# Two-layer trunk: one packed input for the front with three transfers in flight, a third raw buffer, rotating low halves, and the first norm in the fifth chunk

## The chip, the cores and the metric

The kernel runs on one core of one Trainium2 chip. The metric is the device time of one execution in microseconds (us). One profiled execution of the kernel before is read row by row; its times count from the start of its span. The engines are called by the names of the profile: PE is TensorE (matmuls; PEld is its weight load), DVE is VectorE, ACT is ScalarE, POOL is GpSimd, SP is SyncE, which here issues nearly all DMA transfers.

## The reference

The kernel computes a two-layer trunk on 256 tokens with 16 meta tokens ahead of them (272 positions), model width 2048, in float32:

```python
h = concat([meta, x])                                   # 272 x 2048
for i in range(2):
    hn = rms_norm(h, pre_norm_g[i])
    y = diff_attention(hn) if i == 0 else pool_mixer(hn)
    h = h + rms_norm(y, post_norm_g[i])
return h[16:]
# diff_attention: proj = hn @ w_in (2048 -> 8192: q, k, v, gate); 8 heads, two softmax maps each,
#   p1 - lam * p2, per-head norm, times silu(gate), @ w_out (2048 -> 2048)
# pool_mixer: proj = hn @ w_in (2048 -> 4096: u, gate); windowed means minus u, a grouped
#   512 x 512 matmul, times silu(gate), @ w_out
```

`rms_norm` divides by the root of the mean square over the 2048 features and scales by a learned vector.

## The kernel before

**Layout and arithmetic.** Activations lie transposed: features on the 128 partitions, 16 feature blocks (k = 0 to 15), 272 positions in the free dimension. Each float32 operand of a matmul is split into a high half (a cast to the reduced type float32r) and a low half (value minus high half); a product is then three matmuls: high by high, high by low, low by high (`mm3`, L119). Weights are read in chunks of 128 x 2048 (1 MB, `CW` = 2048): one chunk is 128 output features with all 16 k blocks. `load(i)` (L75) issues chunk i's transfer on SP into a ring of two raw buffers, `split(i)` (L84) makes the high half on ACT (L97) and the low half on DVE (L98), `take()` (L110) hands out chunk i, splits i + 1 and loads i + 2.

**The front.** The first four chunks (`FIRST`) are not read one after the other. They are packed with the activations: `first` has for each k the 272 activation columns and 4 x 128 weight columns (784 columns, 392 KB for one k). SP issues eleven pieces of it, all at once as far as its queue goes: k = 0 in two pieces (400 and 384 columns), k = 1, 2, 3 alone, then pairs (L216 to L219). The small table `sp` of learned vectors (70 columns, 35 KB) has a transfer of its own, issued by ACT (L140). For every k, ACT casts the weights (`fhi`, L243) and scales and casts the activations (`xs`, L247), DVE makes the low halves (`flo`, L244; the low part of `xs`, L248), and PE runs 12 matmuls: four chunks by three (L252 to L254), which accumulate in four banks `pq0` to `pq3`. I call the 12 matmuls of one k a slice. Before the data is there, PE runs a warm-up on a matrix of ones (`busy(6)`, L206; twelve passes in the trace). The low halves of the first eight k lie in one tile, those of the second eight in another.

**The first norm.** The pre-norm's row factor is applied after the projection, so the projection need not wait for it. ACT squares the activations in place (L237), DVE adds them up by halving (`fold`, L103; 4, 2 and 1 blocks at a time, L107; the sum of both eights at L268). PE then takes the mean over the partitions (`mean`, L177: the tile `rms_pre`), DVE adds epsilon (`v`, L182), POOL raises it to the power −0.5 (L183), DVE lays the result on a diagonal (`r`, L197), PE spreads it over all partitions (`spread`, L198), and DVE copies it out (`r0`, L275). In the kernel before, the mean stands in the sixth chunk (number 5, `pq5`) after 5 of its 16 k blocks, and the spread 25 matmuls later.

**What sets the order.** The program is written as one stream; the framework puts each engine's instructions into a queue of their own, in an order that its scheduler sets from modelled ready times, and adds the semaphores. `issue_after(x)` holds a block's instructions behind x on x's engine. An engine runs its queue strictly in order. A tile taken from a pool with `bufs=n` reuses the memory of the n-th one before it and waits until that is read. Behind the front come the other chunks of the first projection, eight heads of attention between them, the output projection, the second norm with the pooling layer's projections, and the last output with its norm.

Of the kernel before, what the change touches and what calls it, by code (L numbers as in the profile page):

```python
# [42 lines left out]
@with_exitstack  # L43
def trunk(ctx: ExitStack, tc: tile.TileContext, first, hT, xt, small, gpost1, rope, w_in, w_out, p_in, p_grp, p_out, out):
    nc = tc.nc
# [29 lines left out]
    def load(i, parts=1):  # L75
        if i >= NCH or i in raw:
            return
        t = wpool.tile([P, CW], F32, tag="raw", name=f"raw{i}", bufs=2)
        w = CW // parts
        for q in range(parts):  # L80
            nc.sync.dma_start(t[:, q * w:(q + 1) * w], chunks[i][:, q * w:(q + 1) * w])
        raw[i] = t
# [27 lines left out]
    def take(ahead=True):  # L110
        i = cur[0]
        cur[0] += 1
        split(i)
        if ahead:
            split(i + 1)
            load(i + 2)
        return halves[i]
# [14 lines left out]
    def busy(n):  # L132

        ps = bank("busy")
        for _ in range(n):
            pe.matmul(ps[:, 0:P], ones, ones, start=True, stop=True)
# [9 lines left out]
    ones = const.tile([P, P], F32, name="ones")  # L146
    pool.memset(ones, 1.0)
    warm = const.tile([P, 1], F32, name="warm")
    act.square(warm, ones[:, 0:1])
    ones_r = const.tile([P, P], F32R, name="ones_r")  # L150
# [54 lines left out]

    busy(6)  # L206
    x0 = ExitStack()
# [4 lines left out]
    NF = len(FIRST)  # L212
    pk = xp.tile([P, KT, L + NF * P], F32, name="pk")
    fhi = base.tile([P, KT, NF, P], F32R, tag="os", name="fhi")
    flo = (base.tile([P, KT // 2, NF, P], F32R, tag="big", name="flo0"), xp.tile([P, KT // 2, NF, P], F32R, name="flo1"))
    nc.sync.dma_start(pk[:, 0, 0:L + P], first[:, 0, 0:L + P])  # L216
    nc.sync.dma_start(pk[:, 0, L + P:], first[:, 0, L + P:])
    for a, b in ((1, 2), (2, 3), (3, 4), (4, 6), (6, 8), (8, 10), (10, 12), (12, 14), (14, 16)):
        nc.sync.dma_start(pk[:, a:b, :], first[:, a:b, :])  # L219
    load(NF)  # L220
    nc.sync.dma_start(rp, rope)
    load(NF + 1)
    acc0 = [bank(f"pq{i}") for i in range(NF + 2)]
# [15 lines left out]
    for k in range(KT):  # L239
        hi, lw = fhi[:, k], flo[k // 8][:, k % 8]  # L240
        for i, n in ((0, 1), (1, NF - 1)) if k == 0 else ((0, NF),):
            w = pk[:, k, L + i * P:L + (i + n) * P].rearrange("p (i c) -> p i c", c=P)
            act.copy(hi[:, i:i + n], w)  # L243
            dve.tensor_tensor(out=lw[:, i:i + n], in0=w, in1=hi.bitcast(F32)[:, i:i + n], op=ALU.subtract)  # L244
            if i == 0:
                g = sp[:, C_PRE0 + k:C_PRE0 + k + 1]
                act.activation(xh[:, k, :], pk[:, k, 0:L], AF.Copy, scale=g)  # L247
                dve.scalar_tensor_tensor(out=xl[:, k, :], in0=pk[:, k, 0:L], scalar=g, in1=xh.bitcast(F32)[:, k, :],  # L248
                                         op0=ALU.mult, op1=ALU.subtract)
        for i in range(NF):  # L250
            o = acc0[i][:, 0:L]
            pe.matmul(o, hi[:, i], xh[:, k, :], start=k == 0, stop=False)  # L252
            pe.matmul(o, lw[:, i], xh[:, k, :], start=False, stop=False)
            pe.matmul(o, hi[:, i], xl[:, k, :], start=False, stop=k == KT - 1)  # L254
# [32 lines left out]


    lp = const.tile([P, 2], F32, name="lp")
    dve.tensor_tensor(out=lp, in0=sp[:, C_LAM:C_LAM + 2], in1=sp[:, C_LAM + 2:C_LAM + 4], op=ALU.mult)  # L290
    psl = bank("psl")
    pe.matmul(psl[:, 0:2], ones, lp, start=True, stop=True)
    le = const.tile([P, 2], F32, name="le")
    act.activation(le, psl[:, 0:2], AF.Exp)
    dve.scalar_tensor_tensor(out=lamc, in0=le[:, 0:1], scalar=LAM_INIT, in1=le[:, 1:2], op0=ALU.add, op1=ALU.subtract)

# [220 lines left out]
    for slot in range(NH * 6 + KT):  # L517
        if slot < NH * 6:
            h, i = divmod(slot, 6)
            hd = heads[h]  # L520
            if i == 0:
                hd.h = h
                hd.qk = att.tile([P, 4, L], F32, name=f"qk{h}", tag="qk")
                hd.qs = att.tile([P, 2, 4, L], F32R, name=f"qs{h}", tag="qs")
                hd.qkh, hd.qkl = hd.qs[:, 0], hd.qs[:, 1]
                hd.qm = att.tile([P, 2, 2, 32], F32R, name=f"qm{h}", tag="qm")
                hd.sw = att.tile([ROPE, 4, L], F32, name=f"sw{h}", tag="sw")
                hd.vT = att.tile([P, 2, L], F32, name=f"vT{h}", tag="vT")
# [6 lines left out]
        if slot == NF + 2:  # L535
# [147 lines left out]
    def pooled(t, ps):  # L683
# [6 lines left out]
        while step < w:  # L690
# [219 lines left out]
```

## Time and profile before

| what | us |
|---|---|
| median of 3 runs (lowest, highest) | 837.18 (837.1, 837.63) |
| the profiled execution: its own time | 837.1 |
| its span, first to last instruction | 835.3 |
| outside the span | 1.8 |
| PE busy, share of the span | 827.9 (99%) |
| DVE busy | 584.9 (70%) |
| ACT busy | 437.4 (52%) |
| POOL busy | 5.3 (1%) |
| moved by DMA, mean rate | 149.35 MB, 179 GB/s |

PE is busy nearly always, so the few waits of PE matter and the sums of the other engines don't. A row of a timeline gives start, duration, engine, line, operation, tiles (out<-in) and shape; `x6` behind it joins rows that follow each other; in square brackets stand the idle time of the engine ahead of it and what ended it. Durations of matmuls overlap, since they are pipelined: what one costs in a row of equal ones is the distance from start to start. In a row of waits stand the waiting operation, the one waited for, the total, the count and the longest. A row of windows gives for each engine the busy time and, in brackets, the number of instructions.

### The profile page before, as it was taken

What the parts mean: (1) busy time and instruction counts of PE and PEld (TensorE: products, weight loads), DVE (VectorE), ACT (ScalarE), POOL (GpSimd) and SP (SyncE); (2) the same over time, 40 slices, a digit from 0 to 9 for tenths busy, and PEclk for the clock granted to TensorE, in tenths of its full rate; (3) what the DMA queues carried; (4) which work ended last, traced back from release to release, by engine and by line L of the source; (5) the groups of instructions that cost most, each with busy time, mean ns of one, the idle gap of its engine ahead of it and who ended that gap; (6) DMA issues with size and microseconds to landing.
All of it is one profiled execution on the core that took longest, in us unless ns stands there. A gap on an engine that the chain in (4) does not pass through costs nothing.

```text
span 835.3 us, 14459 instructions
## 1 busy us (share of the span) xinstructions
PE 827.9 (99%) x6060; PEld 796.5 (95%) x6060; DVE 584.9 (70%) x962; ACT 437.4 (52%) x681; POOL 5.3 (1%) x13
## 2 busy tenths in 40 slices
PE   9999999999999999999999999999999999999997
PEld 9999999999999999999999999999999888888886
DVE  6799767675868687897854644696998666685523
ACT  8656555454546465855344544654444545563422
POOL 0100000000000000000000000000000000000000
PEclk9999999999999999999999999999999999999999
DMA  9446344444444444345459744146457555545512
GB/s 355 171 151 206 149 157 156 163 160 160 164 153 153 151 151 151 132 179 194 154 189 371 277 179 151 51 176 211 172 204 266 196 190 202 178 174 203 201 50 101
DMA packets 22385, 149.35 MB, mean 179 GB/s; under 512 B 2608, under 2 KB 2992, under 8 KB 5552
## 3 DMA queue, kind: packets, MB, share of 16 engines
q1 hardware_dynamic: 22032, 148.14, 49.0%
q8 instruction: 47, 0.77, 0.4%
q10 hardware_dynamic: 288, 0.30, 0.1%
q14 instruction: 18, 0.15, 0.0%
HBM read 146.33 MB, written 2.10 MB: 178 GB/s over the span
## 4 chain that ended last, share of the span: by engine, by line
PE 98%; POOL 0%; DMA 0%; DVE 0%; ACT 0%; issue 0%; DVEq 0%; ACTq 0%; POOLq 0%
PE p L121 14%; PE p L123 14%; PE p L122 14%; PE pv L129 7%; PE py L121 4%; PE py L123 4%; PE py L122 4%; PE pu L121 4%; PE pu L122 4%; PE pu L123 4%; PE pv L130 4%; PE pz L780 4%; PE pz L779 4%; PE pz L781 3%; PE pm L129 2%; PE pq L252 1%
## 5 line engine op out<-in xcount | busy, mean ns | idle before, releaser
L98 DVE TENSOR_TENSOR lo<-raw,hi 128x2048 fp32r<-128x2048 f32 (+1 forms) x123 | 279.2, 2270 | 137.6 <-ACT hi L97 137.6
L97 ACT CAST hi<-raw 128x2048 fp32r<-128x2048 f32 (+1 forms) x123 | 232.9, 1895 | 188.6 <-PE p L122 96.3
L121 PE MATMUL p<-xs,hi 128*128 128x272 f32 x928 | 270.2, 291 | 0.0
L123 PE MATMUL p<-xs,lo 128*128 128x272 f32 x928 | 268.5, 289 | 0.0
L122 PE MATMUL p<-xs,hi 128*128 128x272 f32 x928 | 267.4, 288 | 0.0
L121 PEld LDWEIGHTS p<-xs,hi 128*128 128x128 f32 x928 | 174.7, 188 | 0.3
L122 PEld LDWEIGHTS p<-xs,hi 128*128 128x128 f32 x928 | 174.8, 188 | 0.0
L123 PEld LDWEIGHTS p<-xs,lo 128*128 128x128 f32 x928 | 174.6, 188 | 0.0
L129 PE MATMUL pv<-hs,hi 128*128 128x512 f32 x256 | 89.5, 393 | 0.0
L121 PE MATMUL py<-os,hi 128*128 128x272 f32 x256 | 74.3, 290 | 0.0
L123 PE MATMUL py<-os,lo 128*128 128x272 f32 x256 | 74.1, 289 | 0.0
L122 PE MATMUL py<-os,hi 128*128 128x272 f32 x256 | 73.7, 288 | 0.0
L130 PE MATMUL pv<-hs,lo 128*128 128x256 f32 x256 | 71.8, 280 | 0.0
L123 PE MATMUL pu<-hs,lo 128*128 128x260 f32 (+3 forms) x224 | 63.7, 285 | 0.0
L121 PE MATMUL pu<-hs,hi 128*128 128x260 f32 (+3 forms) x224 | 63.6, 285 | 0.0
L122 PE MATMUL pu<-hs,hi 128*128 128x260 f32 (+3 forms) x224 | 63.5, 284 | 0.0
L129 PEld LDWEIGHTS pv<-hs,hi 128*128 128x128 f32 x256 | 48.1, 188 | 10.9
L122 PEld LDWEIGHTS py<-os,hi 128*128 128x128 f32 x256 | 48.3, 189 | 0.0
L121 PEld LDWEIGHTS py<-os,hi 128*128 128x128 f32 x256 | 48.2, 188 | 0.0
L123 PEld LDWEIGHTS py<-os,lo 128*128 128x128 f32 x256 | 48.2, 188 | 0.0
L130 PEld LDWEIGHTS pv<-hs,lo 128*128 128x128 f32 x256 | 48.1, 188 | 0.0
L781 PE MATMUL pz<-hi,zs 128*128 128x512 f32 (+1 forms) x120 | 45.0, 375 | 0.0
(254 smaller groups left out, 1318.3 us busy)
## 6 DMA issues: line engine op xcount, KB each, us to landing
raw<-in_w_in SPq DMA_DIRECT2D x60, 1024.0 KB, 4.8
raw<-in_p_in SPq DMA_DIRECT2D x29, 1024.0 KB, 4.8
raw<-in_w_out SPq DMA_DIRECT2D x16, 1024.0 KB, 4.9
raw<-in_p_out SPq DMA_DIRECT2D x14, 1024.0 KB, 4.8
pk<-in_first SPq DMA_DIRECT2D x6, 784.0 KB, 10.6
raw<-in_p_grp SPq DMA_DIRECT2D x4, 1024.0 KB, 4.7
rawu<-in_p_in SPq DMA_DIRECT2D x3, 1024.0 KB, 5.3
h<-in_hT SPq DMA_DIRECT2D x4, 544.0 KB, 7.1
```

The lines of the kernel that those rows point to most:

```text
L97: act.copy(hi[:, s], raw[i][:, s])
L98: rest[i] = dve.tensor_tensor(out=lw[:, s], in0=raw[i][:, s], in1=hi.bitcast(F32)[:, s], op=ALU.subtract)
L121: pe.matmul(o, wh, xh, start=first, stop=False)
L122: pe.matmul(o, wh, xl, start=False, stop=False)
L123: pe.matmul(o, wl, xh, start=False, stop=last)
L129: pe.matmul(ps[:, 0:2 * n], wh, x, start=first, stop=False, skip_group_check=not first)
L130: pe.matmul(ps[:, 0:n], wl, x[:, 0], start=False, stop=last)
L252: pe.matmul(o, hi[:, i], xh[:, k, :], start=k == 0, stop=False)
L779: pe.matmul(ps, zh[:, k, s], wh[:, c], start=k == 0, stop=False)
L780: pe.matmul(ps, zh[:, k, s], wl[:, c], start=False, stop=False)
L781: pe.matmul(ps, zl[:, k, s], wh[:, c], start=False, stop=k == KT - 1)
```

## The change

1. The small table is put ahead of the packed front: `first` becomes one array of 128 x (70 + 16 x 784). Its first piece is 470 columns (table, activations and first weight chunk of k = 0), the second 384, then k = 1 to k = 7 alone and four pairs: thirteen pieces. DVE and ACT read the scale factors of k from there; POOL copies the table to `sp` for later use.
2. Ahead of every piece from the fourth on, POOL copies one column from the piece three places before into the piece's first column. The piece's transfer overwrites that column, so it is issued only after the copy, and the copy runs only after the earlier piece has landed.
3. The raw ring has three buffers in place of two, and `load` runs one chunk further ahead.
4. The low halves of the front's weights rotate through one tile of eight blocks.
5. The fold of the second eight blocks is no longer held behind low half 5; the mean stands in chunk 4 after 8 of its k blocks, and the spread 5 blocks (15 matmuls) later. Low half 5 is held behind the sum of squares, low half 6 behind the copy of `r0`. The matmul for lambda (`psl`) stands between chunks 4 and 5.
6. The matrix of ones is set on DVE instead of POOL, the warm-up is `busy(7)`, and ACT's first activation stands after the pieces.
7. Later: one chunk's halves are split at two places of the slot loop, `prs` shares a ring, and the difference `df` of the pooling layer is written in place.

```diff
-    act.dma_start(sp, small)
+    dve.memset(ones, 1.0)
-        t = wpool.tile([P, CW], F32, tag="raw", name=f"raw{i}", bufs=2)
+        t = wpool.tile([P, CW], F32, tag="raw", name=f"raw{i}", bufs=3)
...
-            load(i + 2)
+            load(i + 3)
...
-    busy(6)
+    busy(7)
...
-    pk = xp.tile([P, KT, L + NF * P], F32, name="pk")
+    pks = xp.tile([P, C_END + KT * (L + NF * P)], F32, name="pk")
+    pk = pks[:, C_END:].rearrange("p (k c) -> p k c", k=KT)
-    flo = (base.tile([P, KT // 2, NF, P], F32R, tag="big", name="flo0"), xp.tile([P, KT // 2, NF, P], F32R, name="flo1"))
-    nc.sync.dma_start(pk[:, 0, 0:L + P], first[:, 0, 0:L + P])
-    nc.sync.dma_start(pk[:, 0, L + P:], first[:, 0, L + P:])
-    for a, b in ((1, 2), (2, 3), (3, 4), (4, 6), (6, 8), (8, 10), (10, 12), (12, 14), (14, 16)):
-        nc.sync.dma_start(pk[:, a:b, :], first[:, a:b, :])
-    load(NF)
-    nc.sync.dma_start(rp, rope)
-    load(NF + 1)
+    flo = base.tile([P, KT // 2, NF, P], F32R, tag="big", name="flo")
+    ends = [0, C_END + L + P] + [C_END + k * (L + NF * P) for k in (1, 2, 3, 4, 5, 6, 7, 8, 10, 12, 14, 16)]
+    for i, (a, b) in enumerate(zip(ends, ends[1:])):
+        if i > 2:
+            pool.tensor_copy(pks[:, a:a + 1], pks[:, ends[i - 3]:ends[i - 3] + 1])
+        with (tc.issue_after(held.ins) if i else ExitStack()):
+            held = nc.sync.dma_start(pks[:, a:b], first[:, a:b])
+    act.square(warm, ones[:, 0:1])
+    pool.tensor_copy(sp, pks[:, 0:C_END])
+    with tc.issue_after(held.ins):
+        load(NF)
+        nc.sync.dma_start(rp, rope)
+        load(NF + 1)
+        load(NF + 2)
...
-                g = sp[:, C_PRE0 + k:C_PRE0 + k + 1]
+                g = pks[:, C_PRE0 + k:C_PRE0 + k + 1]
...
-    split(NF + 1)
-    load(NF + 3)
-    with tc.issue_after(rest[NF + 1].ins):
-        fold(s8[:, 8:KT], s8[:, 8])
-        dve.tensor_tensor(out=sq0, in0=s8[:, 0], in1=s8[:, 8], op=ALU.add)
-    run_part(NF, 0, KT)
-    run_part(NF + 1, 0, 5)
+    fold(s8[:, 8:KT], s8[:, 8])
+    t = dve.tensor_tensor(out=sq0, in0=s8[:, 0], in1=s8[:, 8], op=ALU.add)
+    with tc.issue_after(t.ins):
+        split(NF + 1)
+    load(NF + 4)
+    run_part(NF, 0, 8)
     norm0 = Norm(sq0, "pre0", rcol0).power()
-    with tc.issue_after(norm0.vi.ins):
-        split(NF + 2)
-    run_part(NF + 1, 5, 7)
-    dve.tensor_copy(r0, norm0.spread(r0))
+    run_part(NF, 8, 5)
+    r0c = dve.tensor_copy(r0, norm0.spread(r0))
...
+    run_part(NF, 13, 3)
+    with tc.issue_after(r0c.ins):
+        split(NF + 2)
...
-        df = l1.tile([P, SEQ], F32, tag="df", name=f"df{t}")
+        df = s[:, m - SEQ:m]
```

The scheduler's order on ACT in the front, k = 1 and k = 2 (`fhi` is the cast of the weights, `xs` the scaled activations, `pk<-pk` a square). Before:

```order
L243 CAST fhi<-pk 128x512
L247 ACTIVATE xs<-pk,sp 128x272
L243 CAST fhi<-pk 128x512
L247 ACTIVATE xs<-pk,sp 128x272
L237 ACTIVATE pk<-pk 128x272
```

Now:

```order
L250 CAST fhi<-pk 128x512
L254 ACTIVATE xs<-pk 128x272
L244 ACTIVATE pk<-pk 128x272
L250 CAST fhi<-pk 128x512
L254 ACTIVATE xs<-pk 128x272
```

The square of k = 1 stood behind the cast and scaling of k = 2; now it stands ahead of them.

On DVE around the first norm (`lo_412`, `lo_493`, `lo_562` are low halves 5, 6 and 7; `v_pre`, `r` and the copy of `r` from `rms_pre` are the norm's steps). Before:

```order
L98 TENSOR_TENSOR lo_412<-raw_118,hi_411 128x2048
L107 TENSOR_TENSOR pk<-pk 128x4x272
L107 TENSOR_TENSOR pk<-pk 128x2x272
L168 MEMSET rms_pre_484 128x1
L107 TENSOR_TENSOR pk<-pk 128x272
L268 TENSOR_TENSOR sq_99<-pk 128x272
L182 TENSOR_SCALAR v_pre_489<-rms_pre_484 128x3
L98 TENSOR_TENSOR lo_493<-raw_398,hi_492 128x2048
L197 TENSOR_SCALAR r_87<-ident,rcol_83 128x16
L197 TENSOR_SCALAR r_87<-ident,rcol_83 128x128 x2
L98 TENSOR_TENSOR lo_562<-raw_415,hi_561 128x2048
L275 COPY r_87<-rms_pre_484 128x272
```

Now (`lo_141` is low half 4 in two parts, `lo_430` is 5, `lo_501` is 6):

```order
L107 TENSOR_TENSOR pk<-pk 128x4x272
L236 TENSOR_TENSOR lo_141<-raw_127,hi_140 128x1024 x2
L107 TENSOR_TENSOR pk<-pk 128x2x272
L107 TENSOR_TENSOR pk<-pk 128x272
L166 MEMSET rms_pre_459 128x1
L272 TENSOR_TENSOR sq_98<-pk 128x272
L98 TENSOR_TENSOR lo_430<-raw_130,hi_429 128x2048
L180 TENSOR_SCALAR v_pre_464<-rms_pre_459 128x3
L195 TENSOR_SCALAR r_85<-ident,rcol_81 128x16
L195 TENSOR_SCALAR r_85<-ident,rcol_81 128x128 x2
L279 COPY r_85<-rms_pre_459 128x272
L98 TENSOR_TENSOR lo_501<-raw_132,hi_500 128x2048
```

Low half 5 moved from ahead of the folds to a place between the sum of squares and `v`, and low half 6 from between `v` and `r` to a place behind the copy.

On PE the mean, before in chunk 5 (`pq_125`), row 257 of PE's queue, its spread at row 284:

```order
L122 MATMUL pq_125<-xs,hi_411 128x272
L123 MATMUL pq_125<-xs,lo_412 128x272
L177 MATMUL rms_pre_484<-ones,sq_99 128x1 x2
L177 MATMUL rms_pre_484<-ones,sq_99 16x1
L121 MATMUL pq_125<-xs,hi_411 128x272
```

Now in chunk 4 (`pq_138`), row 218, its spread at row 235:

```order
L122 MATMUL pq_138<-xs,hi_140 128x272
L123 MATMUL pq_138<-xs,lo_141 128x272
L175 MATMUL rms_pre_459<-ones,sq_98 128x1 x2
L175 MATMUL rms_pre_459<-ones,sq_98 16x1
L121 MATMUL pq_138<-xs,hi_140 128x272
```

The mean moved up by 39 rows, and between it and the spread stand 15 matmuls where 25 stood. On POOL three one-column copies, the copy of the table and seven more one-column copies now stand ahead of the two memsets and the first power; on SP the transfers keep their order, with thirteen pieces for eleven and one more chunk load in the front.

More of the change, by code (lines that the diff above doesn't have):

```diff
@@ L43, in trunk @@
 @with_exitstack
-def trunk(ctx: ExitStack, tc: tile.TileContext, first, hT, xt, small, gpost1, rope, w_in, w_out, p_in, p_grp, p_out, out):
+def trunk(ctx: ExitStack, tc: tile.TileContext, first, hT, xt, gpost1, rope, w_in, w_out, p_in, p_grp, p_out, out):
     nc = tc.nc
@@ L139, in trunk @@
     sp = const.tile([P, C_END], F32, name="sp")
-    act.dma_start(sp, small)
     rp = const.tile([P, 2, L], F32, name="rp")
+    ones = const.tile([P, P], F32, name="ones")
+    dve.memset(ones, 1.0)
     ident = const.tile([P, P], F32, name="ident")
@@ L145, in trunk @@
                        base=0, channel_multiplier=1)
-    ones = const.tile([P, P], F32, name="ones")
-    pool.memset(ones, 1.0)
     warm = const.tile([P, 1], F32, name="warm")
-    act.square(warm, ones[:, 0:1])
     ones_r = const.tile([P, P], F32R, name="ones_r")
@@ L239, in trunk @@
     for k in range(KT):
-        hi, lw = fhi[:, k], flo[k // 8][:, k % 8]
+        hi, lw = fhi[:, k], flo[:, k % 8]
         for i, n in ((0, 1), (1, NF - 1)) if k == 0 else ((0, NF),):
@@ L258, in trunk @@
             split_part(NF, slice((k - KT + 2) * (CW // 2), (k - KT + 3) * (CW // 2)))
-    load(NF + 2)
+    load(NF + 3)
     s8 = pk[:, :, 0:L]
@@ L263, in trunk @@
         square0(k)
-    split(NF + 1)
-    load(NF + 3)
-    with tc.issue_after(rest[NF + 1].ins):
-        fold(s8[:, 8:KT], s8[:, 8])
-        dve.tensor_tensor(out=sq0, in0=s8[:, 0], in1=s8[:, 8], op=ALU.add)
-    run_part(NF, 0, KT)
-    run_part(NF + 1, 0, 5)
+    fold(s8[:, 8:KT], s8[:, 8])
[4 more added lines that the diff above has]
+    run_part(NF, 0, 8)
     norm0 = Norm(sq0, "pre0", rcol0).power()
-    with tc.issue_after(norm0.vi.ins):
-        split(NF + 2)
-    run_part(NF + 1, 5, 7)
-    dve.tensor_copy(r0, norm0.spread(r0))
+    run_part(NF, 8, 5)
+    r0c = dve.tensor_copy(r0, norm0.spread(r0))
     dve.tensor_tensor(out=rp[:, 0, :], in0=rp[:, 0, :], in1=r0, op=ALU.mult)
     dve.tensor_tensor(out=rp[0:ROPE, 1, :], in0=rp[0:ROPE, 1, :], in1=r0[0:ROPE, :], op=ALU.mult)
-    run_part(NF + 1, 12, 4)
+    lp = const.tile([P, 2], F32, name="lp")
+    dve.tensor_tensor(out=lp, in0=sp[:, C_LAM:C_LAM + 2], in1=sp[:, C_LAM + 2:C_LAM + 4], op=ALU.mult)
+    run_part(NF, 13, 3)
+    with tc.issue_after(r0c.ins):
+        split(NF + 2)
+    psl = bank("psl")
+    pe.matmul(psl[:, 0:2], ones, lp, start=True, stop=True)
+    le = const.tile([P, 2], F32, name="le")
+    act.activation(le, psl[:, 0:2], AF.Exp)
+    dve.scalar_tensor_tensor(out=lamc, in0=le[:, 0:1], scalar=LAM_INIT, in1=le[:, 1:2], op0=ALU.add, op1=ALU.subtract)
+    run_part(NF + 1, 0, KT)
     x0.close()
@@ L286, in trunk @@
     ssb = att.tile([P, NH, L], F32, name="ssb")
[L289 to L295, printed above, removed]
     sub = const.tile([P, 2], F32, name="sub")
@@ L533, in trunk @@
             proj(ps, 0, L, xh, xl)
-        if slot == NF + 2:
+        if slot == 0:
+            i7 = cur[0] + 1
+            load(i7)
+            halves[i7] = (wpool.tile([P, CW], F32R, tag="hi", name=f"hi{i7}"), wpool.tile([P, CW], F32R, tag="lo", name=f"lo{i7}"))
+            act.copy(halves[i7][0], raw[i7])
+        elif slot == NF:
+            rest[i7] = dve.tensor_tensor(out=halves[i7][1], in0=raw[i7], in1=halves[i7][0].bitcast(F32), op=ALU.subtract)
+        elif slot == NF + 2:
             with tc.issue_after(heads[0].done.ins):
@@ L539, in trunk @@
             split(cur[0] + 1)
-        load(cur[0] + 2)
+        load(cur[0] + 3)
         with tc.issue_after(rest[cur[0]].ins):
@@ L628, in trunk @@
     r1 = l1.tile([P, L], F32, name="r1")
-    prs = l1.tile([P, L], F32, name="prs")
+    prs = l1.tile([P, L], F32, tag="tmp", name="prs", bufs=2)
     def un0(t):
@@ L883 @@
     w_in = _tiles(A(attn_w_in)[0])
+    small = np.concatenate([
+        _cols(A(pre_norm_g)[0]), _cols(A(pre_norm_g)[1]), _cols(A(post_norm_g)[0]), _cols(A(pool_scale)[0]),
+        _cols(A(attn_subln_g)[0]), _cols(A(attn_lambda_q1)[0]), _cols(A(attn_lambda_q2)[0]),
+        _cols(A(attn_lambda_k1)[0]), _cols(A(attn_lambda_k2)[0])], axis=1)
     arrays = {
-        "first": np.ascontiguousarray(np.concatenate(
-            [hT] + [w_in[c].reshape(P, KT, P) for c in FIRST], axis=2)),
+        "first": np.ascontiguousarray(np.concatenate([small, np.concatenate(
+            [hT] + [w_in[c].reshape(P, KT, P) for c in FIRST], axis=2).reshape(P, -1)], axis=1)),
         "hT": hT,
         "xt": np.ascontiguousarray(A(x)[0]),
-        "small": np.ascontiguousarray(np.concatenate([
-            _cols(A(pre_norm_g)[0]), _cols(A(pre_norm_g)[1]), _cols(A(post_norm_g)[0]), _cols(A(pool_scale)[0]),
-            _cols(A(attn_subln_g)[0]), _cols(A(attn_lambda_q1)[0]), _cols(A(attn_lambda_q2)[0]),
-            _cols(A(attn_lambda_k1)[0]), _cols(A(attn_lambda_k2)[0])], axis=1)),
         "gpost1": np.ascontiguousarray(A(post_norm_g)[1:2]),
```

## The prediction

> **What bounds the kernel now.** I read the page first (busy times and the chain of waits), then TensorE's waits, then the busy time by stretches, then the two places with a wait row by row.
>
> ```profile
> span 835.3 us, 14459 instructions
> ...
> PE 827.9 (99%) x6060; PEld 796.5 (95%) x6060; DVE 584.9 (70%) x962; ACT 437.4 (52%) x681; POOL 5.3 (1%) x13
> ...
> PE 98%; POOL 0%; DMA 0%; DVE 0%; ACT 0%; issue 0%; DVEq 0%; ACTq 0%; POOLq 0%
> ```
>
> TensorE is busy 99% of the span and owns 98% of the chain that ended last. No other engine can give time back except by letting TensorE start earlier or wait less. Its waits in the whole run are these:
>
> ```profile
> PE busy L136 <- POOL ones L147: 1.1, 1, 1.1
> PE po L811 <- ACT diag L809: 0.7, 1, 0.7
> PE rms_pre L198 <- DVE r L197: 0.5, 1, 0.5
> PE pq L252 <- ACT xs L247: 0.2, 1, 0.2
> ```
>
> The second row lies in the output stage, which the diff leaves alone. The change can reach the third (the first norm), the fourth and the start. Between them nothing is left to win:
>
> ```profile
> core 0: us, PE busy (x) PEld busy (x) DVE busy (x) ACT busy (x) POOL busy (x), PEclk, DMA share, GB/s
> 8.70:29.70 21.00, 21.00 (x169) 21.00 (x168) 18.60 (x33) 20.22 (x43) 0.00 (x0) 1.00 0.78 315
> 29.80:37.70 7.90, 7.90 (x65) 7.90 (x65) 4.71 (x6) 2.77 (x3) 0.58 (x2) 1.00 0.67 256
> 50.00:825.00 775.00, 774.97 (x5676) 745.25 (x5675) 544.69 (x886) 402.40 (x614) 0.85 (x1) 1.00 0.48 174
> ```
>
> From 8.7 to 29.7 us there are 168 weight loads in 21.0 us: 0.125 us per matmul of 272 columns, 1.51 us for the 12 matmuls of one k slice. From 50 to 825 us TensorE idles 0.03 us. So the third raw buffer, the earlier loads and the in-place difference of the pooling layer have no wait to remove, and I cost them at nothing: 775 us of matmuls cover them. If that cover went, it would show as new TensorE waits there.
>
> The start, row by row on TensorE:
>
> ```profile
> 1.13 2.93 PE L136 MATMUL busy<-ones 128*128 128x128 f32 x12 [1.13 <-POOL ones L147]
> 4.26 0.59 PE L252 MATMUL pq<-xs,fhi 128*128 128x272 f32 x1 [0.20 <-ACT xs L247]
> 4.66 0.43 PE L253 MATMUL pq<-xs,flo 128*128 128x272 f32 x1
> ...
> 6.89 0.28 PE L254 MATMUL pq<-xs,fhi 128*128 128x272 f32 x1
> 7.13 0.65 PE L252 MATMUL pq<-xs,fhi 128*128 128x272 f32 x3
> ...
> 8.76 0.29 PE L252 MATMUL pq<-xs,fhi 128*128 128x272 f32 x1
> ```
>
> Slice 0 starts at 4.26. The ten starts from 4.66 to 6.89 stand 0.223 apart, nearly twice the later 0.125. Slice 1 starts at 7.13, about 0.12 later than one more step of 0.125 would put it (6.89 + 0.12 = 7.01): this is the wait for slice 1's scaled activations. Slice 2 starts at 8.76.
>
> The first norm:
>
> ```profile
> 37.81 0.63 PE L177 MATMUL rms_pre<-ones,sq 128*128 128x1 f32 x6
> ...
> 41.51 0.29 PE L121 MATMUL pq<-xs,hi 128*128 128x272 f32 x1
> 42.29 0.73 PE L198 MATMUL rms_pre<-r,ones 128*128 128x272 f32 x2 [0.49 <-DVE r L197]
> ```
>
> The last of the 25 matmuls between mean and spread starts at 41.51; one step of 0.126 later, at 41.64, the spread could start. It starts at 42.29: **0.65 us is lost here**, more than the wait row says, since the weight load waits too. Removable in all, apart from the start: 0.65 + 0.12.
>
> **The change, part by part.** *The first norm.* Its chain before, and the same chain in the second norm:
>
> ```profile
> 38.48 0.16 DVE L182 TENSOR_SCALAR v_pre<-rms_pre 128x3 f32<-128x3 f32 x1 [3.89 <-PE rms_pre L177]
> 38.56 2.29 DVE L98 TENSOR_TENSOR lo<-raw,hi 128x2048 fp32r<-128x2048 f32 x1
> 41.61 0.62 DVE L197 TENSOR_SCALAR r<-ident,rcol 128x16 f32<-128x16 f32 x3 [0.76 <-POOL rcol L183]
> ```
>
> ```profile
> 38.79 2.79 POOL L183 TENSOR_TENSOR rcol<-v_pre,mhalf 128x3 f32<-128x3 f32 x1 [3.43 <-DVE v_pre L182]
> ```
>
> ```profile
> 566.48 0.85 POOL L183 TENSOR_TENSOR r_pre<-v_pre,mhalf 128x3 f32<-128x3 f32 x1 [524.90 <-DVE v_pre L182]
> ```
>
> The same power of 128x3 values takes 2.79 us once and 0.85 us once. In the first case VectorE runs a 128x2048 low half beside it from 38.56 to 40.85, and the power ends 0.73 after that; in the second case VectorE is idle. The change puts that low half behind the spread's copy, so VectorE idles during the power, and I take 0.85. The chain is then 0.67 (37.81 to 38.48) + 0.31 (to the power's start) + 0.85 + 0.03 + 0.68 (41.61 to 42.29) = 2.54 us. The cover was 41.64 − 37.81 = 3.83 us; with 15 matmuls for 25 it is 3.83 − 10 × 0.126 = 2.57 us. So the chain just fits. One thing can be late next: low half 5 (2.29 us) now stands ahead of the v instruction on VectorE. The mean comes 24 matmuls into chunk 4, at 29.86 + 3.01 = 32.87, and v could go at 33.54. VectorE ended the halves of low half 4 at 28.67; the second four-row fold (1.2), two smaller folds, the sum (1.4 together) and low half 5 (2.2 in a run) now stand there, which gives 33.4: just in time. I allow 0.2 for that. **Term: −0.65 + 0.2 = −0.45**; bounds −0.65 (nothing waits) and +1.3 (the power costs 2.79 whatever runs beside it; rival A).
>
> The Trainium skill, page "SBUF — State Buffer", section "Who interferes with whom", says that a VectorE instruction with two SBUF inputs and a GpSimd instruction that reads SBUF exclude each other, and the later one waits until the other ends. By that rule the 2.79 is a block of 2.06 and a power of 0.73, as the rows suggest, and the term stands; without it, the term is that of rival A.
>
> *The start.* The small table (35 KB) rides in the first transfer, which grows from 200 to 235 KB, and ScalarE issues no DMA. Ten later pieces each wait for a one-column GpSimd copy that reads the piece three before. The rows for sizes, rates and small GpSimd work:
>
> ```profile
> pk<-in_first SPq DMA_DIRECT2D x3, 392.0 KB, 5.0
> ...
> pk<-in_first SPq DMA_DIRECT2D x1, 200.0 KB, 2.7
> pk<-in_first SPq DMA_DIRECT2D x1, 192.0 KB, 2.8
> sp<-in_small ACTq DMA_DIRECT2D x1, 35.0 KB, 2.9
> ```
>
> ```profile
> raw<-in_w_in SPq DMA_DIRECT2D x4, 1024.0 KB, 4.8
> ```
>
> ```profile
> 5.00:10.00 5.00, 5.00 (x33) 4.83 (x32) 3.38 (x7) 3.87 (x9) 0.00 (x0) 1.00 1.03 401
> ```
>
> ```profile
> 1.36 0.29 POOL L151 CAST ones_r<-ones 128x128 fp32r<-128x128 f32 x1
> 1.59 0.10 POOL L153 MEMSET mhalf<- 128x3 f32 x1
> ```
>
> The second of these views is the stretch from 25 to 45 us, where a load of 1 MB is nearly alone: 4.8 us. The first piece: 35 KB more at 401 GB/s is +0.09, and the separate table, which landed last, is gone (−0.16): **term 0**, bounds −0.16 and +0.09. The warm-up has one more pair of passes (0.43 us) and starts up to 0.2 earlier, so it ends near 4.2, still before the data.
>
> Slice 1's piece. Its landing shows on ScalarE:
>
> ```profile
> 6.04 0.62 ACT L243 CAST fhi<-pk 128x512 fp32r<-128x512 f32 x1 [0.83 <-DMA pk<-in_first]
> 6.56 0.52 ACT L247 ACTIVATE xs<-pk,sp 128x272 fp32r<-128x272 f32 x1
> 7.12 0.62 ACT L243 CAST fhi<-pk 128x512 fp32r<-128x512 f32 x1
> 7.64 0.52 ACT L247 ACTIVATE xs<-pk,sp 128x272 fp32r<-128x272 f32 x1
> 8.07 0.41 ACT L237 ACTIVATE pk<-pk 128x272 f32<-128x272 f32 x1
> ```
>
> ```profile
> 6.69 0.69 DVE L244 TENSOR_TENSOR flo<-pk,fhi 128x512 fp32r<-128x512 f32 x1 [1.47 <-ACT fhi L243]
> 7.30 0.49 DVE L248 SCALAR_TENSOR_TENSOR xs<-pk,sp,xs 128x272 fp32r<-128x272 f32 x1
> ```
>
> It landed at 6.0, while several later pieces shared the way. With only three in flight it can land at 5.0 at the earliest (the piece before it at 1.17 + 2.8 = 4.0, plus 0.40 MB at 401 GB/s), and at 6.0 at the latest if the others did not slow it. I take 5.4, nearer the first since fewer share. Slice 1's wait of 0.12 goes: **−0.12**.
>
> *The square moved.* ScalarE did slice 2's cast and scaling right behind slice 1's and the square last; now slice 1's square stands ahead of slice 2's cast, and a square overwrites its input, so it waits for VectorE's low part of slice 1 (the 7.30 row). With T the landing of slice 1's piece: low part ends at T + 1.79 (6.0 to 7.79), square +0.36 (0.32 to 0.41), cast +0.52, scaling +0.53: slice 2 begins at T + 3.2, and its low parts come about 0.32 late for the matmuls that use them (cast to low weights 0.69, low activations 0.49, behind one another). So TensorE gets slice 2 in full at T + 3.52 = 8.92 against the 8.55 at which it would be ready (7.01 + 1.51 + 0.03). **Term: +0.37**, bounds 0 (T = 5.0) and +0.97 (T = 6.0).
>
> *Three in flight.* Slice 2's piece is issued after the first piece (3.5) and a hop: semaphore 0.15, copy 0.10 (the 128x3 memset) to 0.29 (the 128x128 cast), so 0.35. A lone 392 KB takes an estimated 3.2, between 200 KB in 2.7 and 1024 KB in 4.8. It lands at 7.05, before ScalarE is free for it (T + 2.15 = 7.55). The chain on is slice 5 at 7.05 + 0.35 + 3.2 = 10.6, and slices 8–9 (784 KB, an estimated 4.2) at 15.15. TensorE reaches slice 8 at 8.92 + 6 × 1.51 = 17.98 and cast and scaling need 1.1 ahead, so 16.9 would do: 1.7 us in hand over three hops. **Term 0**, bounds 0 and rival B.
>
> **Sum: −0.45 − 0.12 + 0.37 + 0 = −0.20.** The profiled execution took 837.1 (span 835.3 and 1.8 around it), 0.08 under the median of the three runs, 837.18. Forecast: 837.18 − 0.20 = **837.0 us**: no change that can be told.
>
> **Rivals.**
>
> *A, the first power is slow by itself.* The first use costs 2.79 whoever runs beside it. For it: it is the first of only two. Against it: it ends 0.73 behind the low half. The chain is then 2.54 + 1.94 = 4.48 against a cover of 2.57: wait 1.91, 1.26 more than before. −0.12 + 0.37 + 1.26 = +1.5: **838.7**.
>
> *B, slower: the copies are held up behind VectorE.* Like the power at 38.79, a copy may wait for a running two-input instruction; a low-part pair is 0.69 + 0.49 = 1.2 us. With 1.2 more per hop slice 2 lands at 8.25, is complete at 8.25 + 1.05 + 0.32 = 9.62 (stall 1.07), and slices 8–9 land at 18.75, usable at 19.85 against 9.62 + 9.06 = 18.68 (stall 1.17). −0.45 − 0.12 + 1.07 + 1.17 = +1.7: **838.9**. It decides from about 0.6 per hop (1.7 over three). Against it: VectorE has gaps until 17 us (18.6 busy of 21.0). The rule of the Trainium skill cited above (page "SBUF — State Buffer") speaks for this rival, as the copies read SBUF.
>
> *C, faster: the first pieces come clearly earlier.* If the first piece lands 0.5 earlier and slice 1's at 4.7, slice 2 is ready at 8.2 (−0.35 against 8.55), the slow stretch of matmuls is partly paid while waiting, and the norm waits for nothing: −0.12 − 0.35 − 0.65 = −1.1: **836.1**; with 0.6 more at slice 2, 835.5. Against it: slice 2 hangs on its own piece, issued only after the first one.
>
> *D, nothing arrives:* the early gains and losses are swallowed before chunk 4: **837.2**.
>
> **How the numbers follow.** Forecast 0.58, A 0.14, B 0.17, C 0.09, D 0.02. Own range of the forecast: 836.5 to 837.9 (the bounds of the square's term and 0.2 on either side). The range for 8 in 10 takes in A, B and the near end of C: **836.1 to 839.0**. What a measurement here can tell from no change is 0.2%, 1.67 us: below 835.5 or above 838.85. A and B sit at that edge: half of each is past it, with a little for both at once: slower 0.20. Of C two thirds is past it: faster 0.06. The rest, 0.74, is the same.
>
> **What would show it.** A first power of about 0.85 us with VectorE idle and a spread wait under 0.3 confirm the norm's term; 2.8 us proves rival A. Slice 1's cast near 5.4, a square between it and slice 2's cast, and a TensorE wait of some tenths at slice 2 confirm the next two. Casts that wait for the DMA at slices 5 to 9, and copies longer than 0.3 us, are rival B. The forecast is wrong if TensorE shows any new wait after 50 us, or if the first matmul starts more than 0.3 us off 4.26.

## The result and the profile after

The changed kernel takes 839.82 us (median of 9 runs; the kernel before 837.52 in the same runs, also 9). The ratio of the two is 1.0024, with a 95% interval from 1.0015 to 1.0032: 0.24% slower, about 2.0 us. One of the nine runs of the changed kernel was disturbed (1307.72, at a granted clock of 0.574) and is left out of the ratio; without it they lie between 838.66 and 840.11. The profiled execution is the shortest, 838.66, with a span of 836.9 us: 1.6 us above the span of the kernel before. The medians lie 2.3 us apart, so the rows below account for less than a typical execution loses. The forecast was 837.0, with a range up to 839.0.

The page of the changed kernel, span, busy times and the shares of the chain that ended last:

```profile
span 836.9 us, 14515 instructions
...
PE 828.6 (99%) x6062; PEld 796.5 (95%) x6062; DVE 586.2 (70%) x963; ACT 438.1 (52%) x681; POOL 6.3 (1%) x23
...
PE 95%; DMA 3%; DVE 1%; ACT 0%; issue 0%; POOL 0%; DVEq 0%; POOLq 0%; ACTq 0%
```

PE's share of the chain fell from 98% to 95%, and DMA has 3% where it had none. So the first thing to look for is a transfer that PE waits for. PE's waits of the changed kernel (waiting operation, the one waited for, us in total, times, longest):

```profile
PE pq L259 <- ACT xs L254: 1.5, 2, 0.7
PE busy L136 <- DVE eps L156: 1.1, 1, 1.1
PE po L826 <- ACT diag L824: 0.7, 1, 0.7
```

The row of the first norm is gone; the wait for the scaled activations grew from 0.2 to 1.5 us. PE's timeline shows where:

```profile
4.11 0.60 PE L259 MATMUL pq<-xs,fhi 128*128 128x272 f32 x1
...
7.01 0.65 PE L259 MATMUL pq<-xs,fhi 128*128 128x272 f32 x3 [0.75 <-ACT xs L254]
...
9.52 0.39 PE L259 MATMUL pq<-xs,fhi 128*128 128x272 f32 x1 [0.72 <-ACT xs L254]
9.82 0.39 PE L260 MATMUL pq<-xs,flo 128*128 128x272 f32 x1
...
18.88 0.29 PE L261 MATMUL pq<-xs,fhi 128*128 128x272 f32 x1
19.24 0.39 PE L259 MATMUL pq<-xs,fhi 128*128 128x272 f32 x1
19.55 0.39 PE L260 MATMUL pq<-xs,flo 128*128 128x272 f32 x1
19.96 0.39 PE L261 MATMUL pq<-xs,fhi 128*128 128x272 f32 x1
20.19 0.29 PE L259 MATMUL pq<-xs,fhi 128*128 128x272 f32 x1
...
31.86 0.29 PE L121 MATMUL pq<-xs,hi 128*128 128x272 f32 x1
```

Slice 1 starts at 7.01 (7.13 before), slice 2 at 9.52 (8.76 before), and its next matmul 0.30 later where 0.125 is usual. The 0.75 of idle time ahead of slice 1 is no loss against the kernel before: there the matmuls of slice 0 were still slow at that time. Around 19 us, at slice 8, starts stand 0.23 to 0.41 apart again. The line of chunk 4 begins at 31.86. The same two places in the kernel before, the starts of chunk 4 and of chunk 6:

```profile
29.86 0.29 PE L121 MATMUL pq<-xs,hi 128*128 128x272 f32 x1
...
44.00 0.37 PE L121 MATMUL p<-xs,hi 128*128 128x272 f32 x1
```

and the start of chunk 6 in the changed kernel:

```profile
45.70 0.29 PE L121 MATMUL p<-xs,hi 128*128 128x272 f32 x1
```

Here is the whole account of these two executions. Up to chunk 4 the changed kernel loses 31.86 − 29.86 = 2.00 us: from start to start, slice 2 loses about 1.3 us and slice 8 about 0.8 against an even 0.125, less the 0.12 by which slice 1 starts sooner. From there to chunk 6, the stretch with the first norm, it takes 45.70 − 31.86 = 13.84 us against 14.14: 0.30 won. What comes after wins another 0.1: span against span the loss is 1.6. So the loss is made within the first 20 us, and the 790 us behind chunk 6 change next to nothing.

ACT says why PE waits (the number in brackets is ACT's own idle time and what ended it):

```profile
5.92 0.62 ACT L250 CAST fhi<-pk 128x512 fp32r<-128x512 f32 x1 [0.86 <-DMA pk<-in_first]
6.45 0.52 ACT L254 ACTIVATE xs<-pk 128x272 fp32r<-128x272 f32 x1
7.77 0.43 ACT L244 ACTIVATE pk<-pk 128x272 f32<-128x272 f32 x1 [0.81 <-DVE xs L255]
8.42 0.62 ACT L250 CAST fhi<-pk 128x512 fp32r<-128x512 f32 x1 [0.22 <-DMA pk<-in_first]
...
18.14 0.62 ACT L250 CAST fhi<-pk 128x512 fp32r<-128x512 f32 x1 [0.58 <-DMA pk<-in_first]
```

The cast of slice 1 starts at 5.92, of slice 2 at 8.42 and of slice 8 at 18.14, each as its piece lands. Before the change slice 2 was cast at 7.12, and slice 8 here, with no wait ahead of it:

```profile
15.20 0.61 ACT L243 CAST fhi<-pk 128x512 fp32r<-128x512 f32 x1
```

The moved square (7.77) is over at 8.20, 0.2 us ahead of the landing. It stands in the queue where the prediction put it, but it is not what slice 2 waits for last.

### The profile page after: what moved, and what is told of

Its sections match the earlier page's. It is cut to its first block, busy times and chain, and to the rows that moved or that the text cites. A ratio compares the mean times of both kernels' runs of the same rounds, so it can differ in the third digit from the quotient of the medians.

```text
span 836.9 us, 14515 instructions
## 1 busy us (share of the span) xinstructions
PE 828.6 (99%) x6062; PEld 796.5 (95%) x6062; DVE 586.2 (70%) x963; ACT 438.1 (52%) x681; POOL 6.3 (1%) x23
## 4 chain that ended last, share of the span: by engine, by line
PE 95%; DMA 3%; DVE 1%; ACT 0%; issue 0%; POOL 0%; DVEq 0%; POOLq 0%; ACTq 0%
PE p L121 14%; PE p L123 14%; PE p L122 14%; PE pv L129 7%; PE py L121 4%; PE py L123 4%; PE py L122 4%; PE pu L121 4%; PE pu L123 4%; PE pu L122 4%; PE pv L130 4%; PE pz L795 3%; PE pz L794 3%; PE pz L796 3%; DMA pk<-in_first 3%; PE pm L129 2%
## 5 line engine op out<-in xcount | busy, mean ns | idle before, releaser
L795 PE MATMUL pz<-lo,zs 128*128 128x512 f32 (+1 forms) x120 | 45.0, 375 | 0.0
```

The costliest lines, as they stand in the source:

```text
L795: pe.matmul(ps, zh[:, k, s], wl[:, c], start=False, stop=False)
```

## The experiments

Two theories had to be told apart first. H: the loss comes from holding pieces back, so that slice 2's and slice 8's pieces land late. S: it comes from the square that now stands ahead of slice 2's cast. L, a third, put the loss into the later stages.

**Without the holding copies.** Everything else as changed:

```diff
-        if i > 2:
-            pool.tensor_copy(pks[:, a:a + 1], pks[:, ends[i - 3]:ends[i - 3] + 1])
```

> The changed kernel without the ten copies that hold a piece back until the one three before has landed; everything else as changed (the scheduler then puts the square of slice 1 behind slice 2's scaling again, as before the change). Theory H (the loss is the holding back: slice 2's piece landed at 8.40 us where it landed at 7.09 before, the one of slices 8-9 at 18.1 where it landed at 14.0): pieces land as before, TensorE waits neither at slice 2 nor at slice 8, and the time falls by 2 to 3 us under the changed kernel, to about 836.6 (0.5 us under the kernel before: 0.1 at slice 1, 0.4 at the first norm). Rival S (the square's place): the same here, so this run does not tell H and S apart. Rival L (the later stages lose: third raw buffer, shared rings): stays at 839 or more.

Measured: 836.65 us (before 837.37), ratio 0.9990 (0.9981 to 0.9999). About 3 us under the changed kernel, and as expected to 0.1 us. Its row of PE's waits has the warm-up and the output stage, and nothing in the front:

```profile
PE busy L136 <- DVE eps L156: 1.1, 1, 1.1
PE po L822 <- ACT diag L820: 0.7, 1, 0.7
```

Against the ratio of the changed kernel (1.0024) that is 0.34%: the holding costs about 2.8 us, and the rest of the change gains 0.7 to 0.8. L falls. The front is not quite that of the kernel before: slice 2's piece lands at 7.66 (7.09 before), and its first matmuls start at 8.79, 9.09 and 9.32, not yet 0.125 apart. Two differences were not asked for: slice 1's square is back behind slice 2's scaling, and the scheduler puts the spread 21 matmuls behind the mean, not 15, so the norm is covered more widely than in the changed kernel.

**Held, with the square behind.**

```diff
+        with (tc.issue_after(xa[2].ins) if k == 1 else ExitStack()):
             act.square(pk[:, k, 0:L], pk[:, k, 0:L])
```

(`xa[2]` is the scaling of slice 2.)

> The changed kernel, pieces held back, with the square of slice 1 put behind slice 2's scaling on ScalarE. Theory H: no change from the changed kernel (within 0.3 us of it, 838.7 to 840), since in its profile the square ended at 8.2 us and slice 2's piece landed only at 8.40. Rival S: 0.4 to 0.9 us faster than the changed kernel, slice 2 starts that much earlier than 9.52 us.

Measured: 839.35 us, ratio 1.0025 (1.0015 to 1.0035), not to be told from the changed kernel. With the square out of the way ACT sits idle until the piece lands:

```profile
6.31 0.52 ACT L257 ACTIVATE xs<-pk 128x272 fp32r<-128x272 f32 x1
8.86 0.62 ACT L253 CAST fhi<-pk 128x512 fp32r<-128x512 f32 x1 [2.03 <-DMA pk<-in_first]
```

S falls as the cause of the loss: there is nothing to gain from the square's place while the piece comes at 8.4 to 8.9.

**Not held, with the square ahead.** The square of slice 1 is issued right after its low part, and slice 2's cast is held behind it.

```diff
+            with (tc.issue_after(sq1.ins) if k == 2 else ExitStack()):
                 act.copy(hi[:, i:i + n], w)
```

> The changed kernel without the holding copies, and with the square of slice 1 forced ahead of slice 2's cast, as it stands in the changed kernel. With e1_no_hold and e2_square_behind these are the four combinations of holding and square. Prices by the prediction's own step: slice 1's piece at 5.9 us, low part done at 7.7, square 0.36, cast 0.52, scaling 0.53: slice 2 begins at about 9.1 us where 8.6 would do, 0.5 to 0.9 us slower than e1_no_hold (837.2 to 837.5). If H alone holds and the square costs nothing, the same as e1_no_hold (836.6).

Measured: 836.86 us, ratio 0.9994 (0.9985 to 1.0002). That is 0.2 above the run without holding, and the intervals overlap. It is not quite the order of the changed kernel: the scheduler put slice 2's scaling ahead of the square, and only the cast behind it. In the profiles it takes 30.54 − 7.47 = 23.07 us from slice 1 to chunk 4, and the run without holding 30.35 − 7.06 = 23.29. So in this order the square costs nothing that shows, and the 0.5 to 0.9 that I had put on it did not come; its price in the exact order of the changed kernel, with the piece on time, stays open.

**The holding alone, on the kernel before.** Its eleven pieces, eight copies, nothing else of the change.

```diff
+        if i > 2:
+            pool.tensor_copy(pf[:, a:a + 1], pf[:, ends[i - 3]:ends[i - 3] + 1])
```

> The kernel before with nothing but the holding copies added (its eleven pieces, eight copies, three in flight); the scheduler again puts squares ahead of slice 2's cast, as it does whenever the pieces are held. Theory H: slower than before by 2 to 4 us (839.5 to 841), with casts that wait for the DMA at slices 2, 4 and later; more than the change itself, as the norm's gain is missing. Rival L: no slower than 0.5 us.

Measured: 840.28 us, ratio 1.0032 (1.0020 to 1.0045), 2.7 us slower than before. The holding alone loses more than the whole change. The scheduler put slice 1's square ahead of slice 2's cast here too, and the cast waits 0.80 us for its piece behind it. Of the 3.2 us between the two spans (838.5 and 835.3), 2.1 are there by chunk 4 (31.94 against 29.86), and 1.1 stand behind chunk 6: up to the first matmul into the tile `aA`, in the attention heads, it takes 27.82 us against 26.72.

The starts of chunk 4 show how far one profile can be trusted. In the versions that issue on SP alone and hold three in flight they are 31.86 (the changed kernel), 31.94 (this run) and 32.94 (with the square behind). In the others on SP alone they are 29.86 (before), 30.35 and 30.54 (without holding, square behind and ahead), 30.22 (four in flight, below) and 30.29 and 30.41 (the two runs further down that change only the norm). So these last come out up to 0.7 us apart, and holding to three in flight costs 1.3 us or more in every pair.

**How many in flight.** The changed kernel with one, two and four transfers in flight in place of three (`ends[i - n]` for `ends[i - 3]`, and `if i > n - 1`). One in flight measures a lone transfer.

> The changed kernel with one transfer in flight: every piece alone. Measures the disputed cost by itself, issue to landing: the prediction took 3.2 us for a lone 392 KB and 4.2 for 784 KB. If these held, the holding would have cost nothing with three in flight only if in-flight pieces don't slow each other; e1_no_hold and e5_before_hold say that they do: 4.2 to 5.3 each with three in flight. Expected alone: 2.9 to 3.4 and 3.9 to 4.5; the time rises by 25 to 40 us.

> The same with two in flight. If the pieces share one way of about 425 GB/s and have a fixed part of about 2 us, two in flight take 3.3 to 4.0 for 392 KB and move 200 to 240 GB/s; the time rises by 6 to 12 us over the kernel before.

> The changed kernel with four transfers in flight instead of three (each copy reads the piece four before). Theory H with a rate set by what is in flight: three moved about 300 GB/s, four move about 400, and slice 2's piece is issued with the first ones and lands near 7.4; most of the loss goes: 836.8 to 837.8. If the copies themselves cost (the hop, the lock), the loss stays above 838.5.

Measured: 862.22 us with one and 844.84 with two (one run each), 837.58 with four (ratio 1.0000, 0.9991 to 1.0009). The rows of issue to landing, in us, for the single slices and the pairs: one in flight,

```profile
pk<-in_first SPq DMA_DIRECT2D x4, 784.0 KB, 4.3
...
pk<-in_first SPq DMA_DIRECT2D x7, 392.0 KB, 3.1
```

two in flight,

```profile
pk<-in_first SPq DMA_DIRECT2D x4, 784.0 KB, 5.9
...
pk<-in_first SPq DMA_DIRECT2D x7, 392.0 KB, 3.7
```

three, the changed kernel,

```profile
pk<-in_first SPq DMA_DIRECT2D x4, 784.0 KB, 6.2
...
pk<-in_first SPq DMA_DIRECT2D x7, 392.0 KB, 4.2
```

and four:

```profile
pk<-in_first SPq DMA_DIRECT2D x4, 784.0 KB, 7.3
...
pk<-in_first SPq DMA_DIRECT2D x7, 392.0 KB, 5.0
```

The stretch from 6 to 18 us gives the rate (last number of each row, GB/s): one, two, three, four in flight, the changed kernel without holding, and the kernel before, in this order:

```profile
6.00:18.00 12.00, 7.67 (x37) 6.59 (x38) 3.78 (x7) 4.49 (x9) 0.73 (x4) 0.72 0.40 106
```

```profile
6.00:18.00 12.00, 10.63 (x68) 8.84 (x67) 6.19 (x12) 7.98 (x17) 1.20 (x6) 1.00 0.73 213
```

```profile
6.00:18.00 12.00, 10.53 (x79) 9.86 (x78) 8.20 (x17) 9.29 (x21) 1.89 (x8) 1.00 0.87 285
```

```profile
6.00:18.00 12.00, 11.77 (x90) 11.54 (x89) 9.23 (x18) 10.67 (x24) 2.49 (x8) 1.00 0.95 331
```

```profile
6.00:18.00 12.00, 12.00 (x90) 11.51 (x89) 9.66 (x18) 10.89 (x25) 0.00 (x0) 1.00 1.03 407
```

```profile
6.00:18.00 12.00, 12.00 (x92) 11.82 (x92) 9.70 (x19) 11.50 (x27) 0.00 (x0) 1.00 1.02 417
```

106, 213, 285, 331, 407 and 417 GB/s. A slice is 0.40 MB and PE uses one in 1.51 us, so it needs 266 GB/s on average: three in flight deliver hardly more and make up little of a delay, two do not deliver it. (With one, the granted clock in that stretch was 0.72, the third number from the end, so PE was slower there as well.) With four, slice 2's piece is no longer held and the front keeps one wait of 0.4 us (slice 3). Chunk 4 starts at 30.22 and the norm's stretch to chunk 6 takes 13.45 us, as without holding (30.35 and 13.46). But at 58 us PE waits for DVE:

```profile
58.46 0.40 PE L121 MATMUL p<-xs,hi 128*128 128x272 f32 x1 [0.50 <-DVE e L406]
```

```profile
55.85 2.26 DVE L98 TENSOR_TENSOR lo<-raw,hi 128x2048 fp32r<-128x2048 f32 x1
```

A low half stands ahead of the scores' sums on DVE there. From chunk 6 to the first matmul into `aA` this run takes 27.43 us, the one without holding 26.66: these 0.77 us are more than the difference of the two spans (0.6), and most of the 0.9 us between the medians. A wait at this place shows in the runs with holding alone, with one and with two in flight too, and not in the changed kernel's own profile (26.65); what decides it was not tried.

**Low half 6 ahead of the norm, on the kernel before.** One order changed, so that DVE runs no low half beside the first power.

```diff
-    with tc.issue_after(norm0.vi.ins):
+    with tc.issue_after(sqi.ins):
         split(NF + 2)
```

(`sqi` is the sum of squares.)

> The kernel before with one order changed: low half 6 stands ahead of the norm's v instruction on VectorE, not between v and r, so VectorE is idle while GpSimd takes the first power. Theory P (the power was blocked by the low half beside it): the power takes 0.85 us where it took 2.79, the wait of 0.65 us ahead of the spread goes, time 0.6 us under the kernel before. Rival A (the first power is slow by itself): 2.8 us again, no gain.

Measured: 836.93 us (before 837.59), ratio 0.9992 (0.9983 to 1.0000). The power, and the low half now ahead of it:

```profile
39.22 0.86 POOL L183 TENSOR_TENSOR rcol<-v_pre,mhalf 128x3 f32<-128x3 f32 x1 [3.34 <-DVE v_pre L182]
```

```profile
36.11 2.29 DVE L98 TENSOR_TENSOR lo<-raw,hi 128x2048 fp32r<-128x2048 f32 x1 [1.01 <-ACT hi L97]
38.90 0.16 DVE L182 TENSOR_SCALAR v_pre<-rms_pre 128x3 f32<-128x3 f32 x1 [0.51 <-PE rms_pre L177]
```

0.86 us where it was 2.79: the first power is not slow, it was blocked by the low half beside it. Rival A falls. This is what the Trainium skill, page "SBUF — State Buffer", section "Who interferes with whom", states of an instruction of DVE with two SBUF inputs and one of POOL that reads SBUF; the run agrees. The gain, 0.66 us in the medians, is at the edge of what the interval resolves, but the wait row of the spread is gone from the profile.

**The norm's part alone, on the kernel before.** Fold not held, mean in chunk 4, low half 6 behind the copy.

```diff
-    run_part(NF, 0, KT)
-    run_part(NF + 1, 0, 5)
+    run_part(NF, 0, 8)
     norm0 = Norm(sq0, "pre0", rcol0).power()
...
+    run_part(NF, 8, 5)
```

> The kernel before with the norm part of the change alone: the fold no longer held, mean in chunk 4 after 8 blocks, spread 15 matmuls later, low half 6 behind the copy of r0; transfers, warm-up and raw ring as before. Theory: power 0.85 us, wait ahead of the spread 0 to 0.2, time 0.45 to 0.65 us under the kernel before. If moving the norm costs something elsewhere (low half 6 too late for chunk 6), no gain or a loss.

Measured: 836.92 us, ratio 0.9992 (0.9983 to 1.0001), the same as the run before it. Its power takes 0.86 us. So the norm's move is worth about 0.65 us, and one line that moves low half 6 is worth as much. In this kernel the scheduler put 20 matmuls between mean and spread.

**Versions that might beat both.** All three are without holding and have slice 1's square behind slice 2's scaling. The first has slice 1's piece on ACT's queue; the second is the same with two more pairs of warm-up passes; the third has the second piece on ACT's queue and one more pair. The first one's edit of the transfers:

```diff
-            held = nc.sync.dma_start(pks[:, a:b], first[:, a:b])
+            if i == 2:
+                act.dma_start(pks[:, a:b], first[:, a:b])
+            else:
+                held = nc.sync.dma_start(pks[:, a:b], first[:, a:b])
```

> The changed kernel without the holding copies, square of slice 1 behind slice 2's scaling, and slice 1's piece issued by ScalarE at the start, beside the first piece on SyncE, instead of third on SyncE. If slice 1's piece lands earlier for it (5.9 in e1_no_hold, expected 5.0 to 5.5), slice 1 starts 0.4 to 0.9 us earlier and slice 2's piece too: 835.8 to 836.3. If the pieces only share one way, the first piece comes later by what slice 1 gains: the same as e1_no_hold or up to 0.5 slower.

> e9_k1_on_act with two more pairs of warm-up passes, which fill the gap from 4.2 to 5.0 us ahead of the first matmul. Theory C (the long times of e9_k1_on_act, 837.7 to 838.4 against 836.3 to 836.7 in its other runs, come from the slow spacing that lasted to 9.06 us after that gap): all runs near 836.3, fast spacing by 7 us in the profile. If the two groups of times have another cause, they stay.

> e1_no_hold with the second piece (384 columns) issued by ScalarE beside the first, square of slice 1 behind slice 2's scaling, and one more pair of warm-up passes. In e9_k1_on_act two issuing queues brought slice 2's piece 1.5 us earlier (6.12 us against 7.66) but the first one 0.75 later. If the early pieces are short of issue rather than of rate, the first two land near 3.9, slice 1's near 5.1, slice 2's near 6.1, and slice 2 starts at 7.7 to 8.3 us where it started at 8.8: 835.7 to 836.3. If the slow spacing of the matmuls lasts to 8 or 9 us as in e9_k1_on_act, nothing is won or 1 us lost.

Measured: 837.72 us for the first, with five runs from 836.32 to 836.67 and six from 837.72 to 838.38; 836.59 for the second, all eleven from 836.34 to 836.87, ratio 0.9988 (0.9979 to 0.9997); 836.61 for the third, again in two groups (six from 836.15 to 836.61, five from 837.79 to 838.25). Slices 1 and 2 do come earlier with two queues (slice 2's piece landed 1.0 to 1.5 us earlier than without), but the first piece comes later (4.24 to 4.66 against 3.49). In the profiles of the first and the third, both of the longer group of times, the matmuls also stay slow for longer. In that of the first:

```profile
5.04 0.60 PE L262 MATMUL pq<-xs,fhi 128*128 128x272 f32 x1 [0.63 <-ACT xs L256]
...
9.06 0.42 PE L263 MATMUL pq<-xs,flo 128*128 128x272 f32 x1
9.29 0.32 PE L264 MATMUL pq<-xs,fhi 128*128 128x272 f32 x1
9.45 0.29 PE L262 MATMUL pq<-xs,fhi 128*128 128x272 f32 x1
```

The starts stand 0.23 apart until 9.29 and about 0.125 after. In the second, with longer warm-up, they are fast from 6.8 on, though an idle gap of 0.6 us stands ahead of its first matmul too, and the longer group of times is gone. That the slow spacing makes the two groups is likely but not shown: no execution of the shorter group of the first or third was profiled. The second one's median is no better than that of the plain version without holding (836.65): both beat the kernel before by about 0.1%, and neither can be told from the other. The expected 0.4 to 0.9 us more did not come.

## Why the prediction was wrong

**The step that failed is the term "Three in flight: 0".** Its durations were right for what they said: 3.2 us for a lone 392 KB (measured alone 3.1) and 4.2 for 784 KB (4.3), and a hop of 0.35 (0.27 to 0.34). But I used lone durations in a chain in which three are in flight. With three, the single slices take 4.2 us in the median and the pairs 6.2. The three transfers of the chain, slices 2, 5 and 8–9, took 4.8, 3.1 and 6.0 us where 3.2, 3.2 and 4.2 stood. So slice 2's piece landed at 8.40 where 7.05 was predicted, slices 8–9 at 18.1 where 15.15 was: not 1.7 us in hand but late. A row that I had quoted gave a warning: in the kernel before, the 392 KB pieces took 5.0 us to land in a full queue, and three of 0.40 MB in 5.0 us are 240 GB/s, while the stretch from 5 to 10 us moved 401. This term and those of slice 1's piece and of the square were to give +0.25 together by chunk 4; they gave +2.0 us between the two profiles (31.86 against 29.86), and at least 1.3 against every other profile on SP alone in which pieces are not held to three or fewer.

**Slice 1's piece, −0.12.** The number came (7.01 against 7.13), by luck: the piece landed at 5.9, not at 5.4, 0.1 sooner than before, and the wait for it did not go. It grew from 0.12 to 0.9 us, since slice 0's matmuls went over to the fast spacing at 5.0 us here and only at about 6.9 before. With only two pieces issued behind it, at 3.6 and 4.1 us, the piece hardly came sooner.

**The square moved, +0.37.** It stands where I said, but it ends at 8.20, before the late piece; held back, the runs with it moved and not moved are alike. As the cause of the loss it falls. At slice 2 the two nearly coincide, though: had the piece come on time, this order would have let slice 2's cast start at 8.20 and not at 8.42, so how much of the 1.3 us at slice 2 the square alone would have kept is not shown. At slice 8 no square is in question: its cast waits 0.58 us for the piece.

**The norm, −0.45.** The mechanism was right in each link: the power takes 0.86 us with DVE idle, and low half 5 is what is late next, by more than the 0.2 allowed. The rows of the changed kernel:

```profile
33.72 2.29 DVE L98 TENSOR_TENSOR lo<-raw,hi 128x2048 fp32r<-128x2048 f32 x1
35.92 0.15 DVE L180 TENSOR_SCALAR v_pre<-rms_pre 128x3 f32<-128x3 f32 x1
```

```profile
36.16 0.86 POOL L181 TENSOR_TENSOR rcol<-v_pre,mhalf 128x3 f32<-128x3 f32 x1 [1.59 <-DVE v_pre L180]
```

v follows low half 5 without a gap, and a part of the wait is left (the gain from chunk 4 to chunk 6 is 0.30, not 0.45). The full gain was there with 15 matmuls too: in the version with slice 1's piece on ACT's queue and the longer warm-up, low half 5 is done in time and v waits for the mean,

```profile
33.86 0.16 DVE L180 TENSOR_SCALAR v_pre<-rms_pre 128x3 f32<-128x3 f32 x1 [0.46 <-PE rms_pre L175]
```

and chunk 4 to chunk 6 takes 13.48 us, 0.66 less than before. Mean and spread start 2.56 us apart there, where the prediction's chain has 2.54.

**Rival B** came nearest in time (838.9 against 839.82) and had the right places (slices 2 and 8) for another reason: it blamed copies held up behind DVE. The hop from the first piece's landing (3.31) to slice 2's issue (3.58) took 0.27, less than I took, and all three copies of the chain take 0.18. Its signs appeared all the same, casts that wait for the DMA at slices 6 and 8 and copies over 0.3 us (three of 0.33 to 0.37, off that chain), so they did not tell the two apart. A copy held up behind DVE shows plainly once, at the last copy:

```profile
18.24 0.69 POOL L220 COPY pk<-pk 128x1 f32<-128x1 f32 x1 [2.83 <-DMA pk<-in_first]
```

```profile
17.59 1.29 DVE L107 TENSOR_TENSOR pk<-pk 128x1088 f32<-128x1088 f32 x1 [0.56 <-ACT pk L244]
```

The copy takes 0.69 in place of 0.18 and ends as the fold does, at about 18.9; but PE does not wait for the piece behind it.

**The range** ended at 839.0, just above A and B. For the transfers only the hop was priced as a risk, and no term and no rival had a transfer take longer because others were in flight.

## What to carry to other kernels

A transfer's duration read alone must not be used in a chain where others are in flight: work out the rate as bytes in flight over the duration at that depth, and hold it against what the consumer uses per us. Holding transfers back to make the first ones sooner needs proof that the first ones are slowed by those behind them; here slice 1's piece landed at 5.9 to 6.0 us with seven pieces issued behind it as with two. A change of several parts is best run part by part: about 0.65 us of gain was in one moved instruction, and 2.8 us of loss in ten one-column copies.

## What the runs showed of the hardware that was not expected

- A single piece of 392 KB as third transfer took about 4.3 us from issue to landing whether seven more were issued behind it before it landed (4.38 before) or two (4.26 in the changed kernel), though alone it takes 3.1.
- From 6 to 18 us the rate rises with the number in flight, 106, 213, 285, 331 GB/s for one to four, and reaches 407 only with the queue full. One piece at a time leaves three quarters of that unused.
- The slow spacing of the first matmuls, 0.23 us, ends at different times: at 5.0 us in the changed kernel, at 9.3 with slice 1's piece on ACT's queue and at 10.1 with the second piece there. The last two kernels have two groups of times each, whose medians lie about 1.7 us apart. The rows of windows from 0 to 10 us show a clock of 1.00 all the while. The Trainium skill, page "TensorE: Matmul & The Clock Gate", section "What's actually happening", has PE at half rate until it has been busy for one window of about 3.4 us whose start does not depend on the kernel. That would explain both the groups and the help from a longer warm-up; the runs do not contradict it, but no run here shows the window itself.
